# Fixed places for the steps of the recurrence, four a chunk, with operands made two chunks ahead

## The chip, the cores and the metric

The kernel runs on one core of a Trainium2 chip. The metric is the device time of one execution in microseconds (us); lower is better. Medians of several runs are compared; one further execution was profiled.

## What is computed

Two hybrid layers run one after the other on 512 tokens of width 1024, then a third block (attention and a mixture of experts). A layer projects the normed input, mixes it in three ways (a pooled mixer, a retention, an RWKV-7 time mix), gates each way and merges. The part of the reference that the change touches is the time mix, a recurrence over the tokens with a 64 x 64 state for each of 8 heads:

```python
def step(S, inp):
    r_t, w_t, k_t, v_t, a_t, b_t = inp
    sa = jnp.einsum('bhvk,bhk->bhv', S, a_t)
    S = (S * w_t[:, :, None, :] + sa[..., None] * b_t[:, :, None, :]
         + v_t[..., None] * k_t[:, :, None, :])
    return S, jnp.einsum('bhvk,bhk->bhv', S, r_t)

_, y = lax.scan(step, jnp.zeros((B, H, N, N), jnp.float32), xs)
```

Around it stand the dense products that use most of the time: `proj = h @ w_in`, one product of each way with `w_branch`, and the product with `w_out`, all in float32.

## The kernel before

**Dense tiles.** `mm3` (L312) makes one 128 x 512 output tile. Both factors are split into a high and a low part, so each of the 8 slices of the inner dimension takes three matmuls (L317): 24 a tile, or 12 for the products with `w_branch`, whose inner dimension is half as long. `split` (L300) makes the parts of a weight: `whi` on ScalarE (L306), `wlo` on VectorE or, for some tiles, GpSimd (L309). `rows_of` has its own loop of dense matmuls (L944).

**The side work.** The recurrence is not run token by token but in 8 chunks of 64 tokens, for two halves of 4 heads. It is written as a generator, `rwkv` (L501), whose pieces are put between dense matmuls: after every second slice `mm3` calls `tick(0.5)`, and each whole tick runs the generator to its next `yield`. Half a dense tile (12 matmuls) is so one round of the side work. A round sets where its instructions are *written*; the order in which an engine gets them is set by a scheduler at build time, which moves what it takes to be ready ahead of what it takes to wait. `issue_after` binds one instruction to come behind another; the matmuls of the chain are bound to each other like that (`mm`, L349).

**The parts of the side work**, in order:

- `rwkv_prep(0)` (L553): operands of half 0. It ends in a recursion on VectorE (31 steps of two operations, L668 and L670) that inverts 32 x 32 blocks, a copy on ScalarE (L675), and stores to memory that SP issues (L676, L678).
- `rwkv_chain` for half 0 (chain 1), beside `rwkv_prep(1)`, which makes the operands of half 1 and ends in the same recursion. What a chunk needs of the stores comes back by SP's loads (`gt` L690, `ti` L700).
- chain 2 for half 1, beside `rwkv_out(0)`, then `rwkv_out(1)` (L814: a layer norm, four transposes L822).

**One chunk of a chain** takes these steps, each of which needs the one before through a copy on another engine: the rest of an inverse (L704 to `xx`, L711 back to `gt`), transposes of the operands (L717, L721) with copies `br` and `uv` on ScalarE (L725, L727); products with `q` into `pu`, the chunk's own part beside them (`own`), `uv` on VectorE (L780); the state's increment `pp`, added to the decayed state (`pd` on GpSimd L794, `pbd` on VectorE L795, L797); the output `y` (ScalarE, L808); and the product of the state with the next chunk's operands, from which comes `q` (L767).

**The order in a layer** (`layer`, L1067): projections of the recurrence; then the side work starts, and above it run the dense tiles of the retention (rows of V, then 8 tiles of q and k with `rotary`, L992 to L996), the pooled mixer, branch 0, gates, branch 1, gates; then `self.drain(rs)` runs what is left of the side work, and branch 2 and the output product close the layer. The retention's heads (L1025 to L1062) are a second side work beside the q and k tiles.

Of the kernel before, what the change touches and what calls it, by code (L numbers as in the profile page):

```python
# [14 lines left out]
AF = mybir.ActivationFunctionType  # L15
# [8 lines left out]
C = 64  # L24
NC_ = T // C
# [154 lines left out]
class Layers:  # L180


    def __init__(self, ctx, tc, a, dbg=None):
        self.tc, self.nc, self.a, self.dbg = tc, tc.nc, a, dbg or {}
        nc = tc.nc
# [29 lines left out]
        nc.gpsimd.memset(self.rst, 1.0)  # L215
        nc.gpsimd.memset(self.rst[:, ::C], 0.0)
        self.flip = 0
        self.after = None
        self.early = {}
        self.side = []  # L220
# [127 lines left out]

    def mm(self, *args, **kw):  # L349

        after = kw.pop("after", None)
        if after is None:
            return self.nc.tensor.matmul(*args, **kw)
        with self.tc.issue_after(after.ins):
            return self.nc.tensor.matmul(*args, **kw)

    def tick(self, w=1.0):
        for st in self.side:
# [142 lines left out]
    def rwkv(self, l, t, wa, out):  # L501
        prep = lambda hf: self.rwkv_prep(l, hf, t[hf][0:2], t[hf][2:4], t[hf][4:6], wa)
        ops = yield from prep(0)
        ys, nxt = yield from self.both(self.rwkv_chain(l, *ops), self.late(t, prep))
        (_, ys) = yield from self.both(self.rwkv_out(0, ys, ops[3]), self.rwkv_chain(l, *nxt))
        yield from self.rwkv_out(1, ys, nxt[3])
        out += ops[3] + nxt[3]
# [171 lines left out]
        yield  # L679
        return AR, BK, v, bv, DC, gd, tn  # L680

    def rwkv_chain(self, l, AR, BT, v, bv, DC, gd, tn):
        nc, c = self.nc, self.c
        ident = c["ident"]
        ys = []
        u_of = lambda hd: (hd % 2) * 2 + hd // 2
        def operands(ch):

            gt = self.S("gt", [128, 4, 128], "gt", 2)
            nc.sync.dma_start(gt, gd[:, 4 * ch:4 * ch + 4, :])  # L690
            if type(AR) is list:
                ar = [t[:, ch, :] for t in AR]
            elif ch:
                t = self.S("ca", [128, 2, 128], "ca", 2)
                nc.sync.dma_start(t, AR[:, :, ch, :])
                ar = [t[:, i] for i in range(2)]
            else:
                ar = None
            ti = self.S("ti", [32, 4, 32], "ti", 2)
            nc.sync.dma_start(ti, tn[:, 4 * ch:4 * ch + 4, :])  # L700
            yield
            px = self.RM()
            for u in range(4):
                nc.tensor.matmul(px[32:64, u * 32:u * 32 + 32], gt[0:32, u, 32:64], ti[:, u, :],  # L704
                                 start=True, stop=True)
            xx = self.S("xx", [64, 128], "xx", 2)
            nc.scalar.activation(xx[32:64], px[32:64, :128], AF.Copy)
            yield
            p2 = self.RM()
            for u in range(4):  # L710
                nc.tensor.matmul(p2[0:32, u * 32:u * 32 + 32], xx[32:64, u * 32:u * 32 + 32], gt[32:64, u, 32:64],  # L711
                                 start=True, stop=True)
            nc.vector.tensor_copy(gt[0:32, :, 32:64], p2[0:32, :128].rearrange("p (u t) -> p u t", u=4))
            yield
            pb = self.RM()
            for i in range(2):
                nc.tensor.transpose(pb[:, i * 128:i * 128 + 128], BT[i][:, ch, :], ident)  # L717
            for i in range(2):
                vt = pb[:, 256 + i * 128:384 + i * 128]
                if ch:  # L720
                    nc.tensor.transpose(vt, v[i][:, C * ch - C:C * ch + C], ident)  # L721
                else:
                    nc.tensor.matmul(vt[64:128], v[i][:, :C], ident, start=True, stop=True)
            br = self.S("br", [128, 256], "br", 2)
            nc.scalar.activation(br, pb[:, :256], AF.Copy)  # L725
            uv = self.S("uv", [128, 256], "uv", 2)
            nc.scalar.activation(uv[64:128], pb[64:128, 256:], AF.Copy)  # L727
            return gt, ar, br, uv

        ready, qys = {}, {}  # L730
        gens = {ch: operands(ch) for ch in range(NC_)}

        def step(ch, n=1):

            for _ in range(n):
                try:
                    next(gens[ch])
                except StopIteration as e:
                    ready[ch] = e.value

        def own(ch, hd, after=None):

            if hd == 0:
                qys[ch] = self.P(("qy", "pp")[ch % 2], 1)
            gt, _, _, uv = ready[ch]
            return self.mm(qys[ch][0:64, hd * 64:hd * 64 + 64], gt[64:128, u_of(hd), 0:64],
                           uv[64:128, hd * 64:hd * 64 + 64], start=hd == 0, stop=False, skip_group_check=True, after=after)

        ready[0] = yield from gens[0]
        step(1)  # L750
        m = None
        for hd in range(4):
            m = own(0, hd, m)
        for ch in range(NC_):
            gt, ar, br, uv = ready[ch]
            qy = qys.pop(ch)
            po, pn = self.pbd[ch % 2], self.pbd[(ch + 1) % 2]

            yo = [qy[64:128, 384:512], qy[0:64, 384:512]]
            if ch:  # L760
                for i in range(2):
                    m = self.mm(qy[0:64, i * 128:i * 128 + 128], ar[i][:, 0:64], po[:, i, :],
                                start=False, stop=False, skip_group_check=True, after=m)
                    m = self.mm(yo[i], ar[i][:, 64:128], po[:, i, :],
                                start=i == 0, stop=False, skip_group_check=True, after=m)
            q = self.S("q", [64, 256], "q", 1)
            nc.vector.tensor_copy(q, qy[0:64, :256])  # L767
            last = ch == NC_ - 1
            if not last:
                step(ch + 1)  # L770
            yield
            if not last:
                step(ch + 1, 2)
            pu = self.RM()
            for hd in range(4):
                m = self.mm(pu[0:64, hd * 64:hd * 64 + 64], gt[0:64, u_of(hd), 0:64], q[:, hd * 64:hd * 64 + 64],
                            start=True, stop=True, after=m)
                if not last:
                    m = own(ch + 1, hd, m)
            nc.vector.tensor_copy(uv[0:64], pu[0:64, :256])  # L780
            yield
            pp = qy[:, 256:384].rearrange("p (a b) -> p a b", a=2)
            if not last:
                for i in range(2):
                    for h2 in range(2):
                        s = slice(64 * h2, 64 * h2 + 64)
                        hs = slice(i * 128 + 64 * h2, i * 128 + 64 * h2 + 64)
                        m = self.mm(pp[s, i, :], br[:, hs], uv[:, hs], start=ch == 0 and i == 0 and h2 == 1, stop=True,
                                    skip_group_check=True, after=m)
                pd = self.S("pd", [128, 2, 64], "pd", 1) if ch else None  # L790
                for h2 in range(2):
                    s = slice(64 * h2, 64 * h2 + 64)
                    if ch:
                        nc.gpsimd.tensor_mul(pd[s], po[s, :, s], DC[s, :, ch:ch + 1].to_broadcast([64, 2, 64]))  # L794
                        nc.vector.tensor_add(pn[s, :, s], pd[s], pp[s])  # L795
                    else:
                        nc.vector.tensor_copy(pn[s, :, s], pp[s])  # L797
            for h2 in range(2):
                for i in range(2):
                    hd = 2 * i + h2  # L800
# [123 lines left out]
    def rows_of(self, src, h, tile, scale=None):  # L924
# [3 lines left out]
        for g in range(2):  # L928
# [11 lines left out]
            for tb in range(4):  # L940
                p = self.P()
                for k in range(8):
                    for i, (x, y) in enumerate(((0, 0), (0, 1), (1, 0))):
                        nc.tensor.matmul(p[:, :256], h[x][k][:, tb * 128:tb * 128 + 128],  # L944
                                         parts[y][k // 2][:, k % 2, :], start=k == 0 and i == 0,
                                         stop=k == 7 and i == 2)
# [964 lines left out]
ATT_RATE = 4.0  # L1911
NEX = 5
NOH = 3


# [14 lines left out]
```

## Time and profile before

| | |
|---|---|
| median of 3 runs | 2029.58 us (2028.18 to 2032.1) |
| the profiled execution | 2028.83 us |
| its span in the trace | 2027.0 us |
| PE (TensorE) busy | 1863.2 us, 92% of the span |
| VectorE, ScalarE, GpSimd busy | 54%, 29%, 26% |
| mean granted TensorE clock | 0.948 of full speed |

The span is cut into 40 slices on the profile's page; the rows of PE's busy tenths and of the granted clock (9 is 90% or more) are read from left to right:

```
PE   6899799999995989989999999699999989899997
PEclk9999899999995999999999999599999969899998
```

Each slice is 50.7 us. The clock shows a 5 in slice 13 and again in slice 26, and PE's busy share a 5 and a 6 there: these slices hold the end of the side work in the first layer and in the second. Times in the timeline count from the span's start. [...]

### The profile page before, as it was taken

What the parts mean: (1) busy time and instruction counts of PE and PEld (TensorE: products, weight loads), DVE (VectorE), ACT (ScalarE), POOL (GpSimd) and SP (SyncE); (2) the same over time, 40 slices, a digit from 0 to 9 for tenths busy, and PEclk for the clock granted to TensorE, in tenths of its full rate; (3) what the DMA queues carried; (4) which work ended last, traced back from release to release, by engine and by line L of the source; (5) the groups of instructions that cost most, each with busy time, mean ns of one, the idle gap of its engine ahead of it and who ended that gap; (6) DMA issues with size and microseconds to landing.
All of it is one profiled execution on the core that took longest, in us unless ns stands there. A gap on an engine that the chain in (4) does not pass through costs nothing. (4 is left out here: it accounts for less than half of the span.)

```text
span 2027.0 us, 26408 instructions
## 1 busy us (share of the span) xinstructions
PE 1863.2 (92%) x10178; PEld 1375.1 (68%) x10178; DVE 1096.7 (54%) x2285; ACT 596.5 (29%) x1086; POOL 534.2 (26%) x447
## 2 busy tenths in 40 slices
PE   6899799999995989989999999699999989899997
PEld 2777567777774867777777777487878768444443
DVE  4656896755335455487847422346554546344435
ACT  3332132223321334223323322144334334111112
POOL 1342374536545210123421231130110122100000
PEclk9999899999995989999999999599999969899998
DMA  7424323444431433333144232044422235899981
GB/s 298 135 87 121 91 68 96 143 120 131 138 98 58 140 115 94 117 91 79 57 119 117 84 101 73 17 128 131 156 66 74 73 113 215 324 422 416 404 352 42
DMA packets 103128, 289.03 MB, mean 143 GB/s; under 512 B 31112, under 2 KB 44296, under 8 KB 94808
## 3 DMA queue, kind: packets, MB, share of 16 engines
q1 hardware_dynamic: 97912, 267.40, 38.8%
q0 software_dynamic: 5088, 19.93, 2.6%
q8 instruction: 81, 1.33, 0.3%
q14 instruction: 47, 0.39, 0.1%
HBM read 268.90 MB, written 21.01 MB: 143 GB/s over the span
## 5 line engine op out<-in xcount | busy, mean ns | idle before, releaser
L317 PE MATMUL mm<-hi,whi 128*128 128x512 f32 x1424 | 576.4, 406 | 39.1 <-DVE ry L995 17.0
L317 PE MATMUL mm<-hi,wlo 128*128 128x512 f32 x1424 | 569.0, 400 | 3.1 <-DVE wlo L309 2.3
L317 PE MATMUL mm<-lo,whi 128*128 128x512 f32 x1424 | 569.1, 400 | 0.4 <-DVE lo L482 0.3
L306 ACT ACTIVATE whi<-wst 128x1024 fp32r<-128x1024 f32 (+1 forms) x202 | 193.1, 957 | 564.9 <-PE mm L317 446.9
L317 PEld LDWEIGHTS mm<-hi,whi 128*128 128x128 f32 x1424 | 271.8, 191 | 111.7 <-issue 20.5
L317 PEld LDWEIGHTS mm<-hi,wlo 128*128 128x128 f32 x1424 | 271.6, 191 | 69.8 <-issue 7.1
L317 PEld LDWEIGHTS mm<-lo,whi 128*128 128x128 f32 x1424 | 272.4, 191 | 67.3 <-issue 7.6
L309 DVE TENSOR_TENSOR wlo<-wst,whi 128x1024 fp32r<-128x1024 f32 (+1 forms) x162 | 190.1, 1174 | 156.3 <-ACT whi L306 155.3
L309 POOL TENSOR_TENSOR wlo<-wst,whi 128x1024 fp32r<-128x1024 f32 (+1 forms) x40 | 87.3, 2183 | 313.4 <-ACT whi L306 230.3
L1770 PE MATMUL pp<-eg,xt 128*64 128x512 f32 x512 | 114.5, 599 | 0.2 <-PEq L1820 0.2
L431 POOL TENSOR_TENSOR wad<-wad,cact 128x1024 f32<-128x1024 f32 x32 | 64.9, 2028 | 155.5 <-DMA wad<-wada 152.0
L433 POOL TENSOR_TENSOR wad<-wad 128x512 f32<-128x512 f32 (+2 forms) x96 | 90.4, 942 | 6.5
L1770 PEld LDWEIGHTS pp<-eg,xt 128*64 128x64 f32 x512 | 37.1, 139 | 74.4 <-issue 74.1
L944 PE MATMUL mm<-vhi,hi 128*128 128x256 f32 x256 | 75.8, 300 | 6.3 <-ACT vhi L938 4.1
L876 POOL TENSOR_TENSOR acc<-acc,tg 128x512 f32<-128x512 f32 x32 | 51.8, 1621 | 100.9 <-DVE tg L874 88.5
L944 PE MATMUL mm<-vlo,hi 128*128 128x256 f32 x256 | 75.9, 298 | 0.7 <-DVE vlo L939 0.6
L944 PE MATMUL mm<-vhi,lo 128*128 128x256 f32 x256 | 74.8, 294 | 0.0
L1810 PE MATMUL mm<-y,ohT 128*128 128x512 f32 x256 | 69.2, 409 | 3.2 <-DVE xr L1812 1.6
L1738 POOL DMA_INDIRECT xg<-hx,idx x16 | 15.5, 966 | 205.2 <-DVE xt L1761 150.9
L668 DVE TENSOR_TENSOR tmp<-tt,lt 64x31 f32<-64x31 f32 (+15 forms) x124 | 54.4, 439 | 16.4 <-DMA lt<-gd 13.9
L1795 PE MATMUL ms<-ed,eht 128*64 128x512 f32 x256 | 58.7, 599 | 4.2 <-ACT eht L1785 4.0
L1810 PEld LDWEIGHTS mm<-y,ohT 128*128 128x128 f32 x256 | 44.8, 188 | 23.3 <-DVE xr L1812 13.2
(408 smaller groups left out, 2804.5 us busy)
## 6 DMA issues: line engine op xcount, KB each, us to landing
wst<-win SPq DMA_DIRECT2D x154, 512.0 KB, 3.7
eg<-egu SPq DMA_DIRECT2D x31, 2048.0 KB, 14.2
ed<-edn SPq DMA_DIRECT2D x31, 1024.0 KB, 10.5
wad<-wada SPq DMA_DIRECT2D x48, 512.0 KB, 5.0
wst<-wbr SPq DMA_DIRECT2D x48, 256.0 KB, 2.8
gd<-gs SPq DMA_DIRECT2D x64, 128.0 KB, 1.8
gt<-gd SPq DMA_DIRECT2D x32, 256.0 KB, 3.2
wst<-wout SPq DMA_DIRECT2D x16, 512.0 KB, 3.9
```

The lines of the kernel that those rows point to most:

```text
L306: nc.scalar.activation(hi, w, AF.Copy)
L309: e.tensor_tensor(lo, w, hi.bitcast(F32), op=OP.subtract)
L317: self.nc.tensor.matmul(ps, w[x][:, k, :], h[y][k], start=start and k == 0 and i == 0, stop=stop and k == n - 1 and i == 2)
L431: nc.gpsimd.tensor_tensor(w, w, self.cact.unsqueeze(2).to_broadcast([128, 8, 128]), op=OP.mult)
L433: nc.gpsimd.tensor_add(w[:, :n], w[:, :n], w[:, n:2 * n])
L668: nc.vector.tensor_tensor(t, tt[:, 0:j + 1, j:j + 1].to_broadcast([2 * nu, j + 1, n]), lt[:, j:j + 1, j + 1:].to_broadcast([2 * nu, j + 1, ...
L876: nc.gpsimd.tensor_add(acc[d], acc[d], t)
L944: nc.tensor.matmul(p[:, :256], h[x][k][:, tb * 128:tb * 128 + 128], parts[y][k // 2][:, k % 2, :], start=k == 0 and i == 0, stop=k == 7 an ...
L1738: self.last_row = self.nc.gpsimd.indirect_dma_start(xg, None, self.hx[:, :], bass.IndirectOffsetOnAxis(ap=idx, axis=0))
L1770: nc.tensor.matmul(p[64 * i:64 * i + 64], x[:, k, 64 * i:64 * i + 64], wts[e + i][0][:, k], start=k == 0, stop=k == 7)
L1795: nc.tensor.matmul(py[64 * i:64 * i + 64], ht[:, 128 * k + 64 * i:128 * k + 64 * i + 64], wts[e + i][1][:, k, 512 * c:512 * c + 512], star ...
L1810: nc.tensor.matmul(p, oT[:, 128 * tb:128 * tb + 128], y, start=i == 0, stop=i == len(parts) - 1)
```

## The change

The chain is rewritten with its steps numbered and bound to dense tiles:

- A step of the chain leaves its last matmul in `self.pin`. The next dense matmul (in `mm3` or `rows_of`) takes it through `pinned()` and is issued behind it. So the scheduler can no longer move dense matmuls of later half tiles ahead of a step, nor a step behind them.
- A chunk is four rounds: **A** `pu` with `own` of the next chunk, then `uv`; **B** `pp`, the state's sum, the decayed state `pd` for the next chunk, the output, the second part of the next chunk's inverse, and the loads for the chunk after the next; **C** state times operands, then `q`; **D** the first part of the inverse and the transposes for the chunk after the next.
- The loads and the operands of a chunk are so made two chunks ahead instead of one; loads are written as `gt`, `ti`, `ca`, and the copy to `uv` stands ahead of the copy to `br`.
- Chain 1 begins `CHAIN_WAIT` = 6 rounds after its preparation has ended; chain 2 at once.

The matmuls of a chunk and their sizes are the same. Chain 1 has 40 rounds now and chain 2 has 34.

```diff
+    def pinned(self):
+        m, self.pin = self.pin, None
+        return m
...
-                self.nc.tensor.matmul(ps, w[x][:, k, :], h[y][k], start=start and k == 0 and i == 0,
-                                      stop=stop and k == n - 1 and i == 2)
+                self.mm(ps, w[x][:, k, :], h[y][k], start=start and k == 0 and i == 0,
+                        stop=stop and k == n - 1 and i == 2, after=self.pinned())
...
-        ys, nxt = yield from self.both(self.rwkv_chain(l, *ops), self.late(t, prep))
+        ys, nxt = yield from self.both(self.rwkv_chain(l, *ops, wait=CHAIN_WAIT), self.late(t, prep))
...
+        for _ in range(wait):
+            yield
+        load(0)
+        load(1)
+        yield
+        m = inverse1(0, m)
+        self.pin = m = turned(0, m)
+        yield
         for hd in range(4):
             m = own(0, hd, m)
+        q = right(0)
+        m = inverse2(0, m)
+        self.pin = m = inverse1(1, m)
+        yield
+        self.pin = m = turned(1, m)
+        yield
         for ch in range(NC_):
...
             nc.vector.tensor_copy(uv[0:64], pu[0:64, :256])
-            yield
+            self.pin = m
+            yield
...
+            if not last:
+                m = inverse2(ch + 1, m)
+            self.pin = m
             if ch + 2 < NC_:
-                step(ch + 2)
+                load(ch + 2)
+            yield
...
+            self.pin = m
+            q = right(ch + 1)
+            yield
+            if ch + 2 < NC_:
+                m = inverse1(ch + 2, m)
+                self.pin = m = turned(ch + 2, m)
             yield
...
+CHAIN_WAIT = 6
```

**The order on PE where chain 2 ends, first layer.** The names are those of the code: `mm` is a dense tile, `rm` a small product, `pp` and `qy` the chain's accumulators. Before, these rows begin a stretch of 63 rows without a dense one, up to the branch that follows the `drain`:

```order
L317 MATMUL mm_5056<-lo_5024,whi_5059 128x512
L317 MATMUL mm_5056<-hi_5023,wlo_5060 128x512
L704 MATMUL rm_3565<-ti_3535,gt_3533 32x32 x4
L711 MATMUL rm_3584<-gt_3533,xx_3570 32x32 x4
L717 MATMUL rm_3590<-ident,bk_1483 128x128
L717 MATMUL rm_3590<-ident,bk_1704 128x128
L721 MATMUL rm_3590<-ident,rw_1320 128x128
L721 MATMUL rm_3590<-ident,rw_1386 128x128
L355 MATMUL rm_3599<-q_3563,gt_3412 64x64
L355 MATMUL pp_3601<-uv_3597,gt_3533 64x64
```

Now (steps are on L354 and L356, as the dense matmuls are):

```order
L354 MATMUL mm_4097<-lo_241,whi_4100 128x512
L354 MATMUL mm_4097<-hi_240,wlo_4101 128x512
L356 MATMUL pp_3929<-uv_3911,br_3913 64x64 x4
L356 MATMUL pp_3929<-uv_3911,gt_3854 64x64 x4
L356 MATMUL rm_4131<-gt_3988,xx_4042 32x32 x4
L356 MATMUL mm_4097<-hi_305,whi_4100 128x512
L354 MATMUL mm_4097<-lo_306,whi_4100 128x512
```

The three middle rows are step B of a chunk; behind them come 12 dense matmuls, of which two are shown, then step C. All steps of both chains stand so, and some 770 rows of dense matmuls are left in the layer when chain 2 ends.

**The order on PE where chain 1 begins, first layer.** Before:

```order
L317 MATMUL mm_2340<-hi_227,whi_2343 128x512
L317 MATMUL mm_2340<-lo_228,whi_2343 128x512
L317 MATMUL mm_2340<-hi_227,wlo_2344 128x512
L704 MATMUL rm_1410<-ti_1384,gt_1382 32x32 x4
L565 MATMUL rm_1417<-cst,ksq_1418 128x2 x4
L565 MATMUL rm_1417<-cst,ksq_1424 128x2 x4
L1052 MATMUL ms_2239<-kt_2075,qd_2069 128x128
```

Now:

```order
L584 MATMUL rm_1599<-rw_363,lora_336 128x512
L589 MATMUL rm_1604<-rw_363,lora_336 128x512
L354 MATMUL rm_1643<-ti_1591,gt_1589 32x32
L356 MATMUL rm_1643<-ti_1591,gt_1589 32x32 x3
L356 MATMUL rm_1650<-ident,rw_543 64x128
L356 MATMUL rm_1650<-ident,rw_577 64x128
L356 MATMUL rm_1650<-ident,bk_752 128x128
L356 MATMUL rm_1650<-ident,bk_924 128x128
L356 MATMUL mm_1624<-hi_305,whi_1627 128x512
L354 MATMUL mm_1624<-lo_306,whi_1627 128x512
```

The step with `ti` is the first of the chain. Counted from the same row of both programs (the last product that the recursion waits for), 199 dense matmuls stood ahead of it and 88 do now; in the second layer 205 and 94. Of the preparation of half 1, matmuls that stood behind the chain's start (L565, and the two rows with `lora`) are ahead of it now; of the retention's heads, 16 matmuls that were ahead are behind.

**The order on VectorE inside the recursion of half 0, first layer.** Before (its steps are the rows `tmp` and `tt`):

```order
L281 TENSOR_TENSOR rt_1878<-rt_1878,ry_1876 128x4
L668 TENSOR_TENSOR tmp_1237<-tt_1198,lt_1197 64x156
L309 TENSOR_TENSOR wlo_2344<-wst_2341,whi_2343 128x1024
L283 SCALAR_TENSOR_TENSOR ry_1876<-rt_1878,ry_1876 128x4
L670 TENSOR_TENSOR tt_1198<-tt_1198,tmp_1237 64x26x6
L844 TENSOR_TENSOR sm_1662<-sm_1662,ry_1876 128x512
L668 TENSOR_TENSOR tmp_1237<-tt_1198,lt_1197 64x135
L670 TENSOR_TENSOR tt_1198<-tt_1198,tmp_1237 64x27x5
L668 TENSOR_TENSOR tmp_1237<-tt_1198,lt_1197 64x112
```

Now:

```order
L597 SCALAR_TENSOR_TENSOR cum_1659<-rst,lw_1601 128x512
L592 TENSOR_SCALAR ag_1606<-ag_1606 128x512
L674 TENSOR_TENSOR tmp_1237<-tt_1198,lt_1197 64x231
L610 TENSOR_SCALAR kg_1700<-ag_1606,pv_104,om_328 128x512
L676 TENSOR_TENSOR tt_1198<-tt_1198,tmp_1237 64x21x11
L611 TENSOR_TENSOR kg_1700<-kg_1700,rw_1254 128x512
L674 TENSOR_TENSOR tmp_1237<-tt_1198,lt_1197 64x220
L676 TENSOR_TENSOR tt_1198<-tt_1198,tmp_1237 64x22x10
L605 COPY DC_1454<-cum_1659 128x8
L612 TENSOR_TENSOR bk_1610<-kg_1700,di_1663 128x8x64
L674 TENSOR_TENSOR tmp_1237<-tt_1198,lt_1197 64x207
```

The rows between the steps are now those of half 1's preparation (`cum`, `ag`, `kg`, `DC`, `bk`), where `wlo` and a layer norm stood. Over the whole recursion 22 rows of that preparation have come in, and three rotary tiles (three rows each), three `wlo` and two large rows of the retention have gone out. GpSimd's order moves likewise: the five operations of half 1 on L593, L601 and L621 (L599, L607 and L627 now) stood behind the end of this recursion and stand inside it now.

## Rows read from the trace of the kernel before

**Rows 1.** Stretches: us, busy us of PE, PEld, DVE, ACT, POOL, PEclk, DMA share, GB/s.
```profile
247.00:440.00 193.00, 181.14 (x1099) 138.41 (x1097) 142.58 (x285) 59.05 (x101) 95.29 (x80) 0.97 0.37 110
593.00:652.00 59.00, 34.28 (x267) 26.55 (x265) 28.18 (x68) 11.22 (x29) 30.68 (x31) 0.60 0.23 72
1256.00:1314.00 58.00, 34.74 (x277) 25.66 (x275) 21.04 (x64) 11.75 (x30) 6.96 (x10) 0.62 0.08 24
```

**Rows 2.** The dense matmuls (L317) alone in the two tails.
```profile
593.00:652.00 59.00, 8.79 (x27) 5.77 (x25) 0.60 0.23 72
1256.00:1314.00 58.00, 10.52 (x33) 6.82 (x31) 0.62 0.08 24
```

**Rows 3.** Timeline of PE around the first tail: start us, us, engine, line, operation.
```profile
598.26 0.39 PE L317 MATMUL mm<-lo,whi 128*128 128x512 f32 x1
598.49 0.39 PE L317 MATMUL mm<-hi,wlo 128*128 128x512 f32 x1
```

**Rows 4.** Timeline of PE behind the first tail.
```profile
646.65 1.22 PE L317 MATMUL mm<-hi,whi 128*128 128x512 f32 x2 [2.74 <-ACT hi L328]
...
651.26 0.39 PE L317 MATMUL mm<-lo,whi 128*128 128x512 f32 x1
```

**Rows 5.** Timeline of PE around the start of chain 1, first layer.
```profile
233.95 0.66 PE L1062 MATMUL ms<-ident,sm 128*128 128x128 f32 x4 [3.18 <-DVE sm L844]
...
238.35 0.61 PE L1050 MATMUL ms<-v,sm 128*128 128x128 f32 x4
...
246.63 0.43 PE L704 MATMUL rm<-ti,gt 32*32 32x32 f32 x8
246.99 1.95 PE L565 MATMUL rm<-cst,ksq 128*128 128x2 f32 x16
...
256.10 1.12 PE L578 MATMUL rm<-rw,lora 64*128 64x512 f32 x2
```

**Rows 6.** Timeline of SP, both layers, the load of the first inverse.
```profile
240.72 6.67 SPq L700 DMA_DIRECT2D ti<-tn  x3
...
929.12 4.48 SPq L700 DMA_DIRECT2D ti<-tn  x3
```

**Rows 7.** DMA issues: KB each, median us from issue to landing.
```profile
ti<-tn SPq DMA_DIRECT2D x32, 16.0 KB, 2.0
```

**Rows 8.** Timeline of PE, start of chain 1 in the second layer.
```profile
932.83 0.43 PE L704 MATMUL rm<-ti,gt 32*32 32x32 f32 x8
```

**Rows 9.** Groups on VectorE, steps of the preparation: busy, mean ns | idle before, releaser.
```profile
L610 DVE SCALAR_TENSOR_TENSOR rw<-rw,pv,kg 128x512 f32<-128x512 f32 x8 | 8.1, 1016 | 5.0 <-POOL ar L601 5.0
...
L622 DVE TENSOR_TENSOR bk<-rw,di 128x512 f32<-128x512 f32 x8 | 7.4, 920 | 6.6 <-POOL rw L621 6.6
...
L586 DVE TENSOR_SCALAR ag<-ag 128x512 f32<-128x512 f32 x8 | 5.8, 731 | 6.6 <-ACT ag L585 6.6
...
L613 DVE SCALAR_TENSOR_TENSOR rw<-rm,rw 128x512 f32<-128x512 f32 x8 | 5.5, 688 | 6.8 <-PE rm L612 6.8
```

**Rows 10.** Groups on VectorE while the first recursion runs (181 to 237 us).
```profile
L309 DVE TENSOR_TENSOR wlo<-wst,whi 128x1024 fp32r<-128x1024 f32 x6 | 8.8, 1461 | 0.9 <-ACT whi L306 0.9
...
L992 DVE TENSOR_TENSOR rx<-mm,cos 128x512 f32<-128x512 f32 x5 | 3.4, 674 | 0.0
```

**Rows 11.** Timeline of VectorE inside that recursion.
```profile
208.81 0.41 DVE L668 TENSOR_TENSOR tmp<-tt,lt 64x252 f32<-64x252 f32 x1
209.26 2.49 DVE L670 TENSOR_TENSOR tt<-tt,tmp 64x252 f32<-64x252 f32 x1
```

**Rows 12.** Timeline of GpSimd at the same place.
```profile
208.94 2.54 POOL L309 TENSOR_TENSOR wlo<-wst,whi 128x1024 fp32r<-128x1024 f32 x1 [2.00 <-ACT whi L306]
```

**Rows 13.** Timeline of PE at a late copy of chain 1.
```profile
388.61 0.22 PE L355 MATMUL pp<-uv,gt 64*64 64x64 f32 x1
...
394.91 0.52 PE L355 MATMUL qy<-uv,br 128*64 128x64 f32 x8 [3.01 <-DVE uv L780]
```

**Rows 14.** Timeline of VectorE at the same place.
```profile
394.45 0.41 DVE L780 COPY uv<-rm 64x256 f32<-64x256 f32 x1
```

More of the change, by code (lines that the diff above doesn't have):

```diff
@@ L217, in __init__ @@
         self.flip = 0
+        self.pin = None
         self.after = None
@@ L728, in operands @@
[L728 to L741, printed above, removed]
+                    m = self.mm(vt[64:128], v[i][:, :C], ident, start=True, stop=True, after=m)
+            for i in range(2):
+                m = self.mm(pb[:, i * 128:i * 128 + 128], BT[i][:, ch, :], ident, op=nc.tensor.transpose, after=m)
@@ L743, in own @@
+            uv = uvs[ch] = self.S("uv", [128, 256], "uv", 2)
+            nc.scalar.activation(uv[64:128], pb[64:128, 256:], AF.Copy)
+            br = brs[ch] = self.S("br", [128, 256], "br", 2)
+            nc.scalar.activation(br, pb[:, :256], AF.Copy)
+            return m
+        def own(ch, hd, m):
             if hd == 0:
                 qys[ch] = self.P(("qy", "pp")[ch % 2], 1)
[L745 to L747 removed]
@@ L749, in rwkv_chain, with right @@
-        ready[0] = yield from gens[0]
-        step(1)
-        m = None
+            return self.mm(qys[ch][0:64, hd * 64:hd * 64 + 64], gts[ch][64:128, u_of(hd), 0:64],
+                           uvs[ch][64:128, hd * 64:hd * 64 + 64], start=hd == 0, stop=False, skip_group_check=True,
+                           after=m)
+        def right(ch):
+            q = self.S("q", [64, 256], "q", 1)
+            nc.vector.tensor_copy(q, qys[ch][0:64, :256])
+            return q
+        outs = lambda ch: [qys[ch][64:128, 384:512], qys[ch][0:64, 384:512]]
@@ L757, in rwkv_chain @@
             po, pn = self.pbd[ch % 2], self.pbd[(ch + 1) % 2]
[L759 to L765, printed above, removed]
@@ L787, in rwkv_chain @@
                         hs = slice(i * 128 + 64 * h2, i * 128 + 64 * h2 + 64)
-                        m = self.mm(pp[s, i, :], br[:, hs], uv[:, hs], start=ch == 0 and i == 0 and h2 == 1, stop=True,
-                                    skip_group_check=True, after=m)
-                pd = self.S("pd", [128, 2, 64], "pd", 1) if ch else None
+                        m = self.mm(pp[s, i, :], brs[ch][:, hs], uv[:, hs], start=ch == 0 and i == 0 and h2 == 1,
+                                    stop=True, skip_group_check=True, after=m)
                 for h2 in range(2):
@@ L797, in rwkv_chain @@
                         nc.vector.tensor_copy(pn[s, :, s], pp[s])
+                if ch + 2 < NC_:
+                    pd = self.S("pd", [128, 2, 64], "pd", 1)
+                    for h2 in range(2):
+                        s = slice(64 * h2, 64 * h2 + 64)
+                        nc.gpsimd.tensor_mul(pd[s], pn[s, :, s], DC[s, :, ch + 1:ch + 2].to_broadcast([64, 2, 64]))
+            yo = outs(ch)
             for h2 in range(2):
@@ L943, in rows_of @@
                     for i, (x, y) in enumerate(((0, 0), (0, 1), (1, 0))):
-                        nc.tensor.matmul(p[:, :256], h[x][k][:, tb * 128:tb * 128 + 128],
-                                         parts[y][k // 2][:, k % 2, :], start=k == 0 and i == 0,
-                                         stop=k == 7 and i == 2)
+                        self.mm(p[:, :256], h[x][k][:, tb * 128:tb * 128 + 128],
+                                parts[y][k // 2][:, k % 2, :], start=k == 0 and i == 0,
+                                stop=k == 7 and i == 2, after=self.pinned())
                     if k % 4 == 3:
```

71 lines of the change are left out of this document (34 added, 37 removed).

## The prediction

> **What bounds the kernel now.** I read the page first. PE is busy 92% of the span, so what can be won is PE's idle time, PE at the lower of its two clock levels, and matmuls that are not needed; the change removes no matmul. The row of the granted clock then shows where to look: two slices at half, one in each layer. Third, busy time by stretch [rows 1]: in the two tails, 59 and 58 us long, PE is busy 34.3 and 34.7 us at a mean granted clock of 0.60 and 0.62, against 0.97 in the middle of the first layer. There PE does the last chunks of chain 2 one after the other and waits for a copy at every step. Fourth, what dense work lies in the tails: 27 and 33 matmuls [rows 2]. The timeline of PE gives the pitch of dense matmuls at the full clock, 598.49 - 598.26 = 0.23 us [rows 3].
>
> VectorE (54%) is not the bound over the span, but it is in one place. While it runs the recursion of half 0, the chain cannot start, and what PE has to do meanwhile is what the order puts ahead of the chain's first step.
>
> The profiled execution took 2028.83 us, 0.75 below the median of 2029.58; I put the sum onto the median. About 0.2% (4 us) is what a measurement of this kernel can tell from no change.
>
> **Part 1: the tails go.** In the new order every step of chain 2 stands between 12 dense matmuls, and some 770 rows of dense ones are left when it ends, so the stretch of 63 bare rows disappears. What the tails still cost is their work: the dense part, 27 x 0.23 = 6.2 us and 33 x 0.23 = 7.6 us; and the chain's own PE time, which is the busy time that is not dense at the clock it had: (34.28 - 8.79) x 0.60 = 15.3 us and (34.74 - 10.52) x 0.62 = 15.0 us [rows 1, 2]. Gain: 59 - 6.2 - 15.3 = 37.5 and 58 - 7.6 - 15.0 = 35.4, together **72.9 us**. The copies of these steps lie beside 12 dense matmuls (2.8 us), longer than a copy of 0.4 us [rows 14] and its two hand-overs while VectorE is free; it is, in chain 2.
>
> **Part 2: the front opens.** The pin works in the other direction as well. The first step of chain 1 needs the inverse, and the dense matmul that follows it in the program is now bound behind it. Ahead of that step 111 dense matmuls fewer stand in the first layer (199 - 88), and as many in the second (205 - 94). PE comes there earlier and waits. What was done under cover of the recursion must be done later, with nothing else to hide it: 111 x 0.23 = 25.5 us. Sixteen matmuls of the retention's heads go behind too, 5.0 us as they ran (233.95 to 238.96) [rows 5]. Half 1's products come ahead in exchange: one group on L565 (1.95) and six of the kind at 1.12 us, 8.7 us [rows 5]. Net 25.5 + 5.0 - 8.7 = 21.8 us a layer.
>
> The start itself moves. VectorE gets 22 operations of half 1 between the recursion's steps; four such groups have a mean of 0.84 us [rows 9], so 18.5 us. It loses three `wlo` at 1.46, nine rotary operations and two of the retention at about 0.67 [rows 10], 11.8 us. The recursion ends 6.7 us later. Before, there was some slack: the inverse's load is issued at 240.72 and at 929.12 [rows 6], lands 2.0 us later [rows 7], and PE starts on it at 246.63 [rows 5] and 932.83 [rows 8]; slack 3.9 and 1.7 us. So the chain starts 2.8 and 5.0 us later. Loss 24.6 and 26.8, together **51.4 us**. If the recursion took no longer than before, the loss would be 13.4 us less; that is the lower end.
>
> SP's queue is not late here: its stores wait for ScalarE's copy, and the loads of weights ahead of them are fewer. The weights of tiles that were put off are split during the wait, at no cost.
>
> **Part 3: PE's clock behind the wait.** The trace of before shows no long wait of PE in the front. Behind the tail PE comes back at the lower level and stays there from 646.65 to 651.26 [rows 4]; at half the clock half of that time is lost, 2.3 us. I take it once a layer, **4.6 us**. Below, it is nothing; above, chain steps run slow too, some 2 us more.
>
> **Part 4: steps that cannot move.** Before, the scheduler could put dense matmuls between two steps as long as a copy was late. Now each gap is fixed at 12 dense matmuls (step A to B, `pu` to `uv` to `pp`: 2.8 us). In chain 1 VectorE runs the second recursion, and there a `uv` copy came late: its products ended at 388.83, the copy ran at 394.45 and PE idled 3.0 us [rows 13, 14]. Each of chain 1's 16 `uv` copies in two layers can wait so. Below, none more than now; above, most of them. Half 1's preparation is largely done before chain 1 now, so VectorE is freer; I take one more, **3.0 us**. Step C to A has two rounds, and the loads, issued at B for D, two as well (5.5 us against the 2.0 of [rows 7]); these I cost at nothing. If VectorE or SP's queue ran later than that, PE would wait for them as it does for `uv`.
>
> Sum: 72.9 - 51.4 - 4.6 - 3.0 = 13.9 us gained, 2029.58 - 13.9 = **2015.7 us**.
>
> **Rivals.**
>
> *A freer middle.* Between 247 and 440 us PE is idle 193 - 181.1 = 11.9 us in the first layer [rows 1], the 3.0 us for VectorE's `uv` [rows 13] among them. With half 1's preparation already made, these waits can vanish, and with parts 3 and 4 at nothing the time is 2015.7 - 11.9 - 4.6 - 3.0 = 1996 us. Against it: the rotary tiles and `wlo` that left the recursion are then due in that stretch.
>
> *Half 1's preparation makes VectorE wait inside the recursion.* Its operations need results of PE, ScalarE and GpSimd; the four groups of [rows 9] waited 25.0 us in four preparations, 6.25 each. VectorE keeps its order, so the recursion's steps queue behind them. That adds 12.5 us: 2028 us, no change. For it: the order now puts these operations among the steps. Against it: steps stand between them and fill some of the wait.
>
> *GpSimd holds VectorE up.* A step of the recursion took 2.49 us at 209.26, where the one before took 0.41 [rows 11]; GpSimd's `wlo` ran from 208.94 to 211.48 [rows 12]. Five operations of half 1 on GpSimd move into the recursion, with half as many elements. At half of 2.1 us each that is 5.2 us a layer: 2026 us. Against it: rotary and `wlo` operations on GpSimd leave the same stretch. [...]
>
> *The pins turn against the kernel (slower).* If VectorE's queue holds `uv` copies back as at 394.45 in twelve of chain 1's 16 chunks instead of the one counted, PE idles 11 x 3.0 = 33 us more: 2049 us. It decides from five late copies on (13.9 / 3.0). For it: the gap is fixed at 2.8 us, and a copy stood 5.6 us behind its products. Against it: only one wait of that size was found.
>
> *The change does nothing to the bound.* The tails' work moves, and the wait in front is as long as the tails were: 2029.6 us. The fixed order on PE speaks against equal sizes by chance.
>
> **Chances and range.** The forecast 0.36, with a range of its own from 2002 (recursion no longer) to 2028; freer middle 0.14; VectorE's waits 0.18; GpSimd 0.08; pins slower 0.18; nothing 0.06. Faster by over 0.2% (below 2025.5): 0.33 of the forecast, 0.14, 0.05 of the waits and 0.04 of GpSimd, 0.56. Within it: 0.03, 0.09, 0.03 and 0.05, 0.20. Slower: 0.18, 0.04 and small rests, 0.24. The range that should hold 8 in 10 runs from 1995, where the freer middle ends, to 2047; it leaves out half of the slower rival and what lies below 1995.
>
> **What would show it.** Right: no half-clock slice at the end of the side work, chain 2's steps between dense matmuls, and one wait of PE of over 20 us ahead of the first product with `ti` in each layer, with a low clock there. Part 2 is wrong if that wait is short, part 4 if PE shows idle time before `pp` on `uv` in chunk after chunk. The end of the recursion, later by some 7 us against the last product it waits for, tells the second and third rival from the forecast. A time above 2034 or below 2002 would make the forecast wrong.

## The result, and the profile after

The change makes the kernel slower: 2044.72 us (2043.52 to 2046.01) against 2030.62 us in the same runs, a ratio of 1.0071 (95% interval 1.0053 to 1.0088). The forecast was 2015.7 us. The time lies inside the range; the sign is wrong.

The page of the changed kernel: PE's busy time, then PE's busy tenths and the granted clock in 40 slices of 51 us.

```profile
PE 1862.0 (91%) x10178; PEld 1364.9 (67%) x10178; DVE 1088.7 (53%) x2285; ACT 591.8 (29%) x1086; POOL 549.4 (27%) x447
...
PE   6899498999999989967999999999999999899996
...
PEclk9999598999999989978899999999999969899998
```

PE is busy as long as before (1862.0 against 1863.2 us), while the span is 2043.2 instead of 2027.0 us: the whole loss is idle time of PE, 181.2 against 163.8 us. The half-clock slices at the end of the side work are gone; instead there is a 5 in slice 5, where PE stands ahead of chain 1, and 7, 8 and 8 in slices 18 to 20, which hold the same place of the second layer and the beginning of its chain 1.

The same stretches of both kernels, cut at the same instructions: from the last product that the recursion needs to the first product with `ti` (the front), from there to the first `ti` of chain 2 (chain 1), and from there to the last output transpose (chain 2), for the first layer and then the second. Columns are the stretch's length and the busy us of PE, PEld, VectorE, ScalarE and GpSimd, then PEclk. Before:

```profile
174.10:246.60 72.50, 57.01 (x257) 46.53 (x257) 60.17 (x116) 14.61 (x16) 29.32 (x18) 0.91 0.33 90
246.60:475.00 228.40, 216.54 (x1316) 166.30 (x1315) 159.50 (x312) 70.31 (x121) 116.79 (x95) 0.98 0.37 112
475.00:643.70 168.70, 146.55 (x945) 115.44 (x941) 66.36 (x134) 43.91 (x84) 90.10 (x81) 0.88 0.34 106
865.80:932.80 67.00, 58.17 (x264) 47.08 (x263) 55.25 (x115) 14.65 (x16) 22.21 (x14) 0.95 0.33 91
932.80:1147.00 214.20, 212.37 (x1306) 162.32 (x1305) 140.93 (x300) 72.63 (x124) 61.47 (x50) 1.00 0.31 90
1147.00:1305.60 158.60, 138.36 (x902) 107.71 (x898) 51.43 (x121) 42.02 (x82) 30.11 (x28) 0.88 0.24 71
```

After:

```profile
172.80:244.20 71.40, 38.31 (x153) 26.12 (x153) 57.66 (x118) 14.14 (x18) 27.88 (x19) 0.71 0.23 62
244.20:422.10 177.90, 162.35 (x1075) 124.71 (x1075) 127.17 (x277) 49.08 (x91) 80.64 (x65) 0.93 0.33 96
422.10:568.80 146.70, 140.35 (x956) 110.13 (x956) 67.13 (x137) 44.41 (x85) 74.58 (x65) 1.00 0.37 114
864.90:933.30 68.40, 39.24 (x158) 27.11 (x159) 55.51 (x117) 14.03 (x18) 24.35 (x15) 0.75 0.22 58
933.30:1107.70 174.40, 162.56 (x1064) 124.01 (x1065) 116.55 (x271) 49.02 (x91) 49.48 (x41) 0.93 0.28 80
1107.70:1250.30 142.60, 137.15 (x930) 106.00 (x930) 57.32 (x126) 43.78 (x84) 30.11 (x27) 1.00 0.28 83
```

Length less PE's busy time is PE's idle time (us):

| | front | chain 1 | chain 2 |
|---|---|---|---|
| first layer, before | 15.5 | 11.9 | 22.2 |
| first layer, after | 33.1 | 15.6 | 6.4 |
| second layer, before | 8.8 | 1.8 | 20.2 |
| second layer, after | 29.2 | 11.8 | 5.5 |

Chain 2 has 30.6 us less idle time and got PE's full clock (0.88 to 1.00). The front has 37.9 us more, chain 1 13.7 us more, and both lost clock.

**The front.** Timeline of PE in the changed kernel where chain 1 begins (start us, us, what, idle before it):

```profile
244.24 0.28 PE L354 MATMUL rm<-ti,gt 32*32 32x32 f32 x2 [21.99 <-DMA ti<-tn]
...
246.16 0.78 PE L356 MATMUL mm<-hi,whi 128*128 128x512 f32 x1
```

PE waits 22.0 us for the load of the inverse (20.3 us in the second layer), where it came without a wait before [rows 5]. The first dense matmul behind the step takes 0.78 us, against 0.39 at a granted clock of 1.00 [rows 3]: here the granted clock is 0.50, from 244.2 to 250.2. It has two levels in this trace: of 4080 stretches of 0.5 us, 3632 show 1.00, 414 show 0.50, and the 34 between lie where it changes. The load was issued here, first layer and second:

```profile
241.29 3.88 SPq L700 DMA_DIRECT2D ti<-tn  x3
```

```profile
930.50 11.29 SPq L700 DMA_DIRECT2D ti<-tn  x4
```

That is 68.5 and 65.6 us behind the start of the stretch, against 66.6 and 63.3 before [rows 6]: 1.9 and 2.3 us later.

The recursion of half 0 itself, from the second operation of its first step to the end of its last step, first layer and second (columns as above). Before:

```profile
183.64:236.55 52.91, 38.70 (x176) 31.43 (x175) 50.56 (x99) 9.22 (x11) 20.81 (x13) 0.89 0.27 80
873.29:921.68 48.39, 41.56 (x185) 33.35 (x183) 46.36 (x100) 9.14 (x11) 12.62 (x8) 0.93 0.24 71
```

After:

```profile
180.26:237.20 56.94, 30.86 (x113) 19.64 (x112) 55.62 (x114) 10.57 (x15) 20.88 (x14) 0.70 0.15 45
872.73:926.32 53.59, 31.37 (x116) 20.28 (x114) 52.23 (x112) 10.46 (x15) 19.65 (x11) 0.74 0.11 34
```

It takes 4.0 and 5.2 us longer. Counted from the start of the front it ends 1.9 us later in the first layer and 5.5 us in the second. In the second layer SP had issued the load 7.4 us behind the recursion's end before and issues it 4.2 us behind it now, so that only 2.3 us of the 5.5 are left.

**The wait that I had not seen.** Groups of PE, the changed kernel, by line and operation: busy and mean ns, then the idle time ahead of the group and what ended it. `qy` and `pp` are the accumulators of even and odd chunks; `uv,gt` with an end on `pbd` is the output product yo.

```profile
L356 PE MATMUL qy<-uv,gt 64*64 64x64 f32 (+1 forms) x256 | 19.0, 235 | 7.7 <-DVE pbd L802 6.3 <-DVE pbd L804 1.4
L356 PE MATMUL pp<-uv,gt 64*64 64x64 f32 (+1 forms) x256 | 18.8, 238 | 14.1 <-DVE pbd L802 14.1
```

And before:

```profile
L355 PE MATMUL pp<-uv,gt 64*64 64x64 f32 (+1 forms) x256 | 20.3, 250 | 4.6 <-DVE pbd L795 2.3 <-ACT uv L727 2.3
...
L355 PE MATMUL qy<-uv,gt 128*64 128x64 f32 (+1 forms) x248 | 19.2, 247 | 4.4 <-DVE pbd L795 3.1 <-DVE pbd L797 0.8 <-ACT uv L727 0.5
```

PE's wait for the state's sum `pbd` was 2.3 + 3.9 us and is 14.1 + 7.7 = 21.8 us; half of it lies in chain 2, in 14 waits of 0.7 to 1.0 us. A step B in chain 2 shows how, PE and below it VectorE (the four products of a group, `x4` in the program's order, stand in the trace as `x8`):

```profile
455.00 0.45 PE L356 MATMUL pp<-uv,br 128*64 128x64 f32 x8
456.23 0.45 PE L356 MATMUL pp<-uv,gt 128*64 128x64 f32 x8 [0.77 <-DVE pbd L802]
456.61 0.43 PE L356 MATMUL rm<-gt,xx 32*32 32x32 f32 x8
456.97 0.50 PE L356 MATMUL mm<-hi,whi 128*128 128x512 f32 x1
```

```profile
455.57 0.60 DVE L802 TENSOR_TENSOR pbd<-pd,pp 64x128 f32<-64x128 f32 x2 [3.00 <-PE pp L356]
```

`pp` (the state's increment) runs, VectorE adds it to the state, and only then yo runs, 0.77 us later, and the next dense matmul behind that. The new order puts yo directly behind `pp`, and the dense matmul is bound behind both. In chain 1 VectorE is in the second recursion, and its sum comes later:

```profile
339.28 0.45 PE L356 MATMUL pp<-uv,br 128*64 128x64 f32 x8
342.79 0.70 PE L356 MATMUL pp<-uv,gt 128*64 128x64 f32 x8 [3.06 <-DVE pbd L802]
```

```profile
341.01 0.99 DVE L940 COPY ws<-ws 128x4 f32<-128x4 f32 x1
341.92 0.30 DVE L674 TENSOR_TENSOR tmp<-tt,lt 64x156 f32<-64x156 f32 x1
342.15 0.58 DVE L802 TENSOR_TENSOR pbd<-pd,pp 64x128 f32<-64x128 f32 x2
```

The sum is ready to run at 339.7 (`pp`'s end) and starts at 342.15; VectorE is busy until then with the recursion, the retention and the pooled mixer. PE waits 3.06 us, and its granted clock falls from 1.00 to 0.50. Ten us around this wait and around a like one of 4.38 us in the second layer (columns as above):

```profile
340.00:350.00 10.00, 7.21 (x36) 5.42 (x36) 8.99 (x24) 2.10 (x4) 5.82 (x6) 0.66 0.11 28
1027.00:1037.00 10.00, 6.10 (x34) 4.74 (x35) 9.17 (x31) 1.72 (x4) 3.46 (x5) 0.66 0.12 39
```

The granted clock is 0.50 from 342.5 to 349.3 and from 1028.6 to 1035.4, for 6.8 of the ten us each time. PE's other waits of over 1.8 us in the two chain 1s are, but for one of 2.21 us, not for `pbd`: 3.49 and 1.83 us for half 1's preparation (`gs`), 4.92 us for the pooled mixer (`ws`), 2.23 us for the retention (`sm`). A granted clock of 0.50 lay beside each of these four too, for 3.4 us at the two waits for `gs` and 6.8 us at the other two.

### The profile page after: what moved, and what is told of

It reads as the page before. It is cut to its first block, busy times and chain, and to the rows that moved or that the text cites. A ratio compares the mean times of both kernels' runs of the same rounds, so it can differ in the third digit from the quotient of the medians.

```text
span 2043.2 us, 26468 instructions
## 1 busy us (share of the span) xinstructions
PE 1862.0 (91%) x10178; PEld 1364.9 (67%) x10178; DVE 1088.7 (53%) x2285; ACT 591.8 (29%) x1086; POOL 549.4 (27%) x447
## 5 line engine op out<-in xcount | busy, mean ns | idle before, releaser
L354 PE MATMUL mm<-hi,wlo 128*128 128x512 f32 x1424 | 567.5, 399 | 2.0 <-DVE wlo L310 1.5
L354 PE MATMUL mm<-lo,whi 128*128 128x512 f32 x1424 | 567.0, 398 | 0.1
L354 PE MATMUL mm<-hi,whi 128*128 128x512 f32 x1296 | 519.3, 401 | 15.3 <-DVE rw L502 6.2
L354 PEld LDWEIGHTS mm<-hi,wlo 128*128 128x128 f32 x1424 | 272.2, 191 | 69.6 <-issue 4.5
L354 PEld LDWEIGHTS mm<-lo,whi 128*128 128x128 f32 x1424 | 273.0, 192 | 63.7 <-issue 6.5
L354 PEld LDWEIGHTS mm<-hi,whi 128*128 128x128 f32 x1296 | 248.0, 192 | 77.8 <-ACT hi L486 7.8
L439 POOL TENSOR_TENSOR wad<-wad 128x512 f32<-128x512 f32 (+2 forms) x96 | 98.0, 1021 | 6.2
L354 PE MATMUL mm<-vhi,hi 128*128 128x256 f32 x256 | 75.3, 298 | 6.2 <-ACT vhi L970 4.0
L354 PE MATMUL mm<-vlo,hi 128*128 128x256 f32 x256 | 74.9, 295 | 0.7 <-DVE vlo L971 0.6
L354 PE MATMUL mm<-vhi,lo 128*128 128x256 f32 x256 | 74.4, 292 | 0.0
L1770 POOL DMA_INDIRECT xg<-hx,idx x16 | 15.5, 969 | 205.7 <-DVE xt L1793 151.0
L356 PE MATMUL mm<-hi,whi 128*128 128x512 f32 x128 | 65.5, 511 | 0.0
```

The lines of the kernel that those rows point to most:

```text
L354: return op(*args, **kw)
L356: return op(*args, **kw)
L439: nc.gpsimd.tensor_add(w[:, :n], w[:, :n], w[:, n:2 * n])
L1770: self.last_row = self.nc.gpsimd.indirect_dma_start(xg, None, self.hx[:, :], bass.IndirectOffsetOnAxis(ap=idx, axis=0))
```

## The experiments

Two edits stand in several of them. **yo first** moves the four output products ahead of the four of `pp`, inside the same step, and moves the flag that begins the accumulation with them:

```diff
+            yo = outs(ch)
+            for h2 in range(2):
+                for i in range(2):
+                    hd = 2 * i + h2
+                    m = self.mm(yo[i][:, 64 * h2:64 * h2 + 64], gt[:, u_of(hd), 64:128], uv[:, hd * 64:hd * 64 + 64],
+                                start=ch == 0 and i == 0 and h2 == 0, stop=h2 == 1, skip_group_check=True, after=m)
             pp = qy[:, 256:384].rearrange("p (a b) -> p a b", a=2)
...
-            yo = outs(ch)
...
```

**No pin** makes `pinned()` return None, so that no dense matmul is bound to a step.

### 1. A longer wait ahead of chain 1

```diff
-CHAIN_WAIT = 6
+CHAIN_WAIT = 16
```

> The only edit is CHAIN_WAIT = 16 in place of 6. Theory A (front): in the changed kernel PE waits 22 and 20 us for the load of the first inverse because 111 dense matmuls fewer stand ahead of the first step of chain 1; with ten more rounds ahead of it (120 dense matmuls, 27 us) these two waits shrink to under 5 us each, PE's idle time between the last product that the recursion needs and the chain's start goes from 33 and 29 us back to some 15 and 9, and the stretch at the lower clock there goes too: about 45 us gained, near 2000 us. Rival B (the wait only moves): chain 2 starts later by as much and its last steps are bare again: 2030 to 2045 us.

Measured: 2011.86 us, 0.9911 of the kernel before (0.9884 to 0.9937). PE's wait at the chain's start is down to 0.9 us:

```profile
269.73 0.31 PE L354 MATMUL rm<-ti,gt 32*32 32x32 f32 x2 [0.90 <-DVE gs L646]
```

The front's wait is a cost of its own and does not come back at the end: chain 2 has 6.3 and 5.7 us of idle time, as in the changed kernel. It brought 33 us, not 45: PE now waits at other places of the longer front for half 1's preparation, 6.1 us ahead of L618 in the first layer and 7.0 us ahead of a dense tile in the second, the two longest.

### 2. yo first

> The only edit is inside step B: the four output products (yo) are issued ahead of the products pp instead of behind them, so that they no longer follow the read of the same accumulator by VectorE's sum (pbd). CHAIN_WAIT stays 6. Theory A: in the changed kernel yo stands directly behind pp with no dense matmul between and waits for pbd in every chunk, 14.1 + 7.7 = 21.8 us of idle time, and three of these waits are followed by the lower clock; all of that goes: 2044.7 - 22 to 26, about 2020 us. Rival B: PE waits for pbd one step later instead, since VectorE is late by itself: 2040 us or more.

Measured: 2010.48 us, 0.9905 (0.988 to 0.993). Step B in chain 2, timeline of PE:

```profile
447.02 0.45 PE L356 MATMUL pp<-uv,gt 128*64 128x64 f32 x8
447.30 0.40 PE L356 MATMUL pp<-uv,br 128*64 128x64 f32 x8
447.63 0.43 PE L356 MATMUL rm<-gt,xx 32*32 32x32 f32 x8
448.00 0.50 PE L356 MATMUL mm<-hi,whi 128*128 128x512 f32 x1
```

There is no idle time between the rows; PE's wait for `pbd` is left at 2.1 us in the whole kernel. Chain 1 and chain 2 of the first layer, then of the second, cut and columns as above:

```profile
244.30:415.70 171.40, 158.60 (x1076) 121.84 (x1076) 127.97 (x277) 48.59 (x91) 80.91 (x65) 0.95 0.32 100
415.70:555.90 140.20, 138.16 (x950) 108.83 (x950) 68.44 (x137) 43.82 (x84) 78.29 (x69) 1.00 0.38 123
918.70:1079.90 161.20, 153.05 (x1063) 118.11 (x1063) 117.66 (x271) 49.09 (x91) 49.30 (x41) 0.98 0.29 87
1079.90:1215.60 135.70, 135.70 (x930) 105.48 (x930) 57.21 (x126) 43.87 (x84) 29.60 (x27) 1.00 0.27 87
```

Putting four products in another place is worth 34 us of the changed kernel, more than the 21.8 us of waits. Chain 2 is 6.5 and 6.9 us shorter, with the clock at 1.00 in both kernels. Chain 1 is 6.5 and 13.2 us shorter, and its clock rose from 0.93 to 0.95 and 0.98: the lower level behind the two long waits for `pbd` (two, where I had counted three) is gone, that behind some of the other waits is left (behind one of 3.49 us, which ended at 290.93, dense matmuls take 0.63 us, as they do in the changed kernel at a granted clock of 0.50).

### 3. Both

> Both edits together. Theory A: the two costs lie at different places and add up: 2044.7 - 45 - 24, about 1976 us, faster than the kernel before by some 2.6%. Rival B (the wait only moves): the gain of the second edit alone, 2020 us.

Measured: 1986.6 us, 0.9789 (0.9765 to 0.9812). The gains nearly add up (33 + 34 against 58).

### 4. The new chain without binding

> The chain as in the changed kernel, but no dense matmul is bound behind a step (pinned() gives nothing), CHAIN_WAIT 6. Theory A: both costs come from the binding; the scheduler puts dense matmuls ahead of the chain's first step and between pp and yo as before, and since operands are made earlier the bare tail is shorter than before: 1985 to 2005 us. Rival C: the new chain itself (four rounds a chunk, operands two chunks ahead) is what costs, or the binding is what takes the tail away: 2030 us or more.

Measured: 2000.72 us, 0.9862 (0.9835 to 0.9888). So the new chain by itself is faster than the old one, and binding it costs 44 us at this place of yo. The tail is shorter, but there. Windows over its two ends, columns as above:

```profile
600.00:645.00 45.00, 30.49 (x159) 23.49 (x157) 24.87 (x45) 10.27 (x18) 32.56 (x25) 0.81 0.30 100
1265.00:1300.00 35.00, 24.31 (x109) 18.56 (x108) 15.26 (x35) 7.46 (x12) 11.64 (x8) 0.80 0.16 54
```

### 5. Binding in chain 2 alone

`pinned()` gives a step only after chain 2 has begun.

> Steps are bound only in chain 2; chain 1 is left to the scheduler, CHAIN_WAIT 6, yo behind pp as in the changed kernel. Theory A: the front's wait comes from binding chain 1 alone, so PE's idle time ahead of the first product with ti is that of the run without bindings (17 to 18 us instead of 33 and 29), the waits for pbd in chain 1 are gone and those of chain 2 stay at 0.8 us a chunk: 1990 to 2005 us. Rival C: the bindings of chain 2 cost as much as those of chain 1; then it stays above 2020 us.

Measured: 2016.76 us, 0.9922 (0.9892 to 0.9952), slower than expected by 12 us and more. Chain 1, unbound, falls behind what is written; when the first step of chain 2 is bound, all that is left of chain 1 has to run ahead of it without dense matmuls. Windows over these two places, which end with the first steps of chain 2 (at 410.7 and 1077.6):

```profile
385.00:415.00 30.00, 22.27 (x185) 17.48 (x182) 11.34 (x38) 6.37 (x20) 15.34 (x15) 0.60 0.38 120
1050.00:1080.00 30.00, 23.63 (x215) 18.36 (x216) 10.58 (x35) 6.05 (x19) 2.22 (x6) 0.54 0.20 62
```

Dense matmuls are busy for 2.3 and 0.4 us of these 30. A bare stretch with PE at 0.60 and 0.54 of the clock is back, in the middle of the layer. The time lies between the two forecasts. The front's idle time is 18.2 and 16.1 us, as A said, and that of chain 2 is 5.8 and 5.5 us, as in the changed kernel; what neither had is this cost of changing from free to bound.

### 6. No pin, yo first

> No dense matmul is bound, and yo stands ahead of pp, CHAIN_WAIT 6. Theory A: without bindings the scheduler already puts dense matmuls between pp and yo, so the new place of yo gains little, 0 to 8 us against the run without bindings (2000.7): 1993 to 2001 us. Rival: yo's place is worth as much as with bindings, some 30 us: 1970 us, and then the binding has no use at all.

Measured: 1965.43 us, 0.9673 (0.9643 to 0.9703), the fastest kernel of the study; the rival was right. The six stretches, cut and columns as above:

```profile
173.50:261.00 87.50, 68.53 (x292) 51.23 (x291) 75.62 (x150) 20.95 (x26) 45.36 (x25) 0.88 0.27 74
261.00:422.80 161.80, 153.33 (x1070) 118.22 (x1069) 121.67 (x255) 48.47 (x90) 80.29 (x68) 1.00 0.39 117
422.80:582.90 160.10, 160.10 (x1058) 128.48 (x1055) 78.91 (x146) 51.97 (x96) 91.10 (x75) 1.00 0.40 123
828.40:914.70 86.30, 69.66 (x297) 53.52 (x297) 73.53 (x149) 20.78 (x26) 34.01 (x21) 0.88 0.26 70
914.70:1074.40 159.70, 157.73 (x1091) 123.11 (x1091) 103.23 (x248) 50.87 (x93) 42.39 (x36) 1.00 0.34 99
1074.40:1229.70 155.30, 155.30 (x1023) 122.87 (x1022) 64.35 (x133) 50.98 (x94) 42.37 (x35) 1.00 0.29 88
```

Chain 2 runs without any idle time at the full clock, with nothing bound. But PE's waits for `pbd` were only 2.7 us in run 4, so the 35 us between the two are not these waits; run 9 comes back to this. The front keeps 19.0 and 16.6 us of idle time, chain 1 8.5 and 2.0 us.

### 7 and 8. Binding with other waits

Both edits of run 3, CHAIN_WAIT 11 and 20.

> Both edits, with CHAIN_WAIT 11 instead of 16. Theory A: 60 dense matmuls more than at 6 stand ahead of the start, half of what is missing; about half of the wait of 22 and 20 us is left: between the 2010 us of 6 rounds and the 1986.6 us of 16, near 1997 us. Rival: the load lands early enough and the wait is gone at 11 already: 1987 us or less.

> Both edits, with CHAIN_WAIT 20. Theory A: the wait for the load of the inverse is gone at 16 already, so four rounds more change nothing, unless the end of chain 2 comes close to the branch that needs it; some 300 dense matmuls are left behind it at 16: 1985 to 1989 us. Rival B: later steps fall on a busier VectorE: 1992 us or more.

Measured: 1995.27 us (0.9822, 0.9791 to 0.9854) and 1979.63 us (0.974, 0.9709 to 0.977). The first is near A's 1997; the second gained 7 us on run 3, where A expected next to nothing. With yo first, 6, 11, 16 and 20 rounds give 2010, 1995, 1987 and 1980 us: later is better as far as was tried, and binding stays behind no binding (1965) even with the front closed.

### 9. The old chain, yo first

> The kernel before with one edit: yo is issued ahead of pp in its chain (three rounds a chunk, operands one chunk ahead, nothing bound). Theory A: PE's waits for pbd in its groups yo (2.3 + 3.9 us) are small, but the order of the chain also frees its later steps, so the bare tails become shorter: 2000 to 2020 us. Rival D: the gain of the unbound new chain comes from operands made two chunks ahead, and yo's place is worth nothing here: 2024 to 2034 us. Should it come near 1965 us, yo's place alone explains the whole gain.

Measured: 1991.77 us, 0.9825 (0.9783 to 0.9867): the same edit gains 1.7% on the kernel before. Neither forecast held: it is worth more than A said and does not explain the 1965 us alone. PE's waits for `pbd` can't explain it: they are 6.2 us before and 4.3 us here. Nor does the chain pass through step B sooner. In the last chunks, with no dense matmul between, the way from the first product of step B to the product with the state takes 1.95 us before (624.51 to 626.46) and 1.90 us here (600.87 to 602.77). What changed is how closely the scheduler put the chunks. In chain 2 of the first layer the products with `br` of four successive chunks begin 27.8 us apart on average before (510.1 to 593.6) and 20.8 us apart here (488.5 to 551.0); between runs 4 and 6 the same distance falls from 22.6 to 17.6 us. So less is left for the tails: chain 2 has 10.7 us of idle time in each layer here, against 22.2 and 20.2 before. Why the build-time order comes out closer with yo first is not shown.

### 10 and 11. No pin, yo first, other waits

> Nothing bound, yo ahead of pp, CHAIN_WAIT 0 in place of 6. Theory A: without bindings the scheduler sets the order, and the wait in rounds only shifts how early the chain is written; the chain ends before the branch that needs it in either case: 1962 to 1970 us. Rival E: the wait of 6 rounds itself helps, since it lets dense tiles go ahead of the chain: 1975 us or more.

> Nothing bound, yo ahead of pp, CHAIN_WAIT 12. Theory A: as for 0, 1960 to 1970 us. Rival E: with a longer wait VectorE's waits in the chain shrink further, 1955 us or less.

Measured with 0 rounds 1969.45 us (0.9698, 0.9663 to 0.9732), with 12 rounds 1966.93 us (0.9691, 0.9656 to 0.9726). With nothing bound the wait decides nothing that can be told here.

### What the parts are worth

| ratio to the kernel before | yo behind pp | yo first |
|---|---|---|
| old chain | 1 | 0.9825 |
| new chain, nothing bound | 0.9862 | 0.9673 |
| new chain, bound, wait 6 (the change: left) | 1.0071 | 0.9905 |

By columns, yo's place is worth 1.7 to 1.9% in each row; by rows, the new chain is worth 1.4 to 1.5% and binding costs 2.1 to 2.3%. The three act almost independently in size. The cause of yo's gain is another in the bound order (waits of PE and the clock, run 2) than in the free ones (a closer order, run 9). The change took the new chain and the binding together, and the binding's cost was larger. Most of that cost is the early start at 6 rounds: with yo first and 20 rounds the bound kernel is 0.7% behind the free one of the same runs (1979.63 against 1965.43 us).

## Why the prediction was wrong, step by step

**What bounds the kernel: right.** The time followed PE's idle time and clock: the 16.2 us of span are the 17.4 us of idle time, less 1.2 us of busy time.

**Part 1, the tails (72.9 us): right in kind.** The bare stretches are gone, chain 2 stands among dense matmuls and the clock stays at 1.00. But a wait came in their place that the sum had not: seven waits for `pbd` of 0.7 to 1.0 us in each chain 2, most of the 6.4 and 5.5 us of idle time left there. Run 2 takes them away.

**Part 2, the front (51.4 us): right, and too large.** PE's wait stands where it was forecast, at 22.0 and 20.3 us, and run 1 shows that it is a cost. The idle time grew by 37.9 us in the two fronts and the clock fell from 0.91 and 0.95 to 0.71 and 0.75. The term of the later start was mis-sized: the chain was to start 2.8 and 5.0 us later, and counted from the start of the front it starts 1.1 us earlier and 1.4 us later. The recursion took 4.0 and 5.2 us longer, against 6.7 by the sum, and the load was issued only 1.9 and 2.3 us later, since the recursion began earlier in the first layer and SP was quicker behind it in the second.

**Part 3, the clock (4.6 us): too small.** A granted clock of 0.50 came not once a layer but beside six of the seven waits of over 1.8 us inside the two chain 1s, whose clock of 0.98 and 1.00 fell to 0.93 in both layers. The reading that the front had no long wait before is wrong as well: at 222.55 us PE had stood 9.16 us for VectorE's `ry`, which is most of that front's 15.5 us of idle time.

**Part 4, steps that cannot move (3.0 us): the step that failed.** It priced the gap from A to B and named `uv`. The trace of the changed kernel shows no wait of PE for VectorE's `uv` in its two layers, where it was 3.9 us before. The gap that mattered is one inside step B, where there is no dense matmul at all: `pp`, the sum on VectorE, yo. The excerpt of the new order shows it, `pp<-uv,br`, `pp<-uv,gt` and `rm<-gt,xx` in neighbouring rows, and a row of the tail before would have shown it too (a wait of 0.77 us at 605.24 us of the kernel before, also for `pbd`). I read those rows as one step and did not ask which of its products reads what another engine still works on. By run 2 that is 34 us, in place of 3.0 in the sum; with it the sum, 13.9 us gained, turns into a loss of 17, against 14 measured. That the two come so close is in part luck: Part 2 was too large, and the sum had nothing for the other waits of chain 1, whose idle time in run 2 is still 20.9 us against 13.7 before the change.

yo waits for VectorE's read of `pp` although the two products write different columns: the accumulator is one tile of 512 float32 columns, with `pp` in columns 256 to 383 and the output in the 128 behind. The trace shows the wait, 0.7 to 1.0 us in chain 2; what makes it necessary no run here shows.

**The rivals.** "The pins turn against the kernel" was right in its kind (a fixed order in chain 1 that meets a busy VectorE) and wrong in its place (`uv` for `pbd`). That its 2049 us lie near the measured time is luck: it had 33 us of waits for `uv` in chain 1, where there are none, and chain 2, where VectorE runs no recursion, has half of the waits for `pbd`. "A freer middle" failed: chain 1's idle time grew. "Half 1's preparation makes VectorE wait" failed: inside the two recursions the trace shows one wait of VectorE, of 0.2 us. "GpSimd holds VectorE up" is not borne out: in the second layer GpSimd was busy 19.7 us beside the recursion, against 12.6 before, and the recursion's own operations took 24.9 us, against 26.3. In the first layer GpSimd's busy time was the same (20.9 against 20.8 us) and they took 32.2 against 30.4 us. The recursions became longer mainly by the operations between the steps.

That the scheduler could do without binding was not among the rivals, since I took the binding as what fills the tail. Run 6 shows that the shorter chain does it: no pin, no tail, 45 us less than the bound chain with the same order (1965 against 2010).

## What to carry to other kernels

When an order is fixed by hand, write down for each step which of its own instructions wait for another engine's reading or writing of the same tile, not only which steps wait for each other; what stands between two of them must be work that does not wait. An instruction that nobody waits for (here the output) goes ahead of the hand-over and not behind it; all three orders tried here gained by that. And before binding dense work to a chain, try the shorter chain without binding: a bound instruction also holds back work that was free to cover an earlier wait.

## What was not expected of the hardware

A wait of PE of 3.06 us in chain 1, and one of 4.38 us, cost more than their length: the granted clock was 0.50 for 6.8 of the ten us around each, and dense matmuls came 0.43 us apart in them, against 0.23 at 1.00. By an estimate from the clock that is up to 3.4 us each on top of the wait (half of 6.8). The waits of 0.7 to 1.0 us in chain 2 left the granted clock at 1.00. In between the length alone did not decide: a wait of 2.21 us that ended at 384.02 was followed by ten us at a granted clock of 1.00, one of 2.23 us that ended at 987.57 by ten us at 0.66.
